# The second norm's factor moved behind the MLP's squares, and the last eighth of w_down without seven-product steps

## The chip, the core and the metric

The kernel runs on one core of a Trainium2 chip. Its engines work side by side, each through its own queue in order: TensorE (PE, with PEld for its weight loads), VectorE (DVE), ScalarE (ACT), GpSimd (POOL) and SyncE (SP), which here only issues loads. Waits between them are semaphores that the framework places from the program's reads and writes; the kernel fixes the order of each queue itself (`manual_schedule`). The metric is the time of one execution in microseconds on the device; the time before is 2056.29 us, the median of three runs from 2054.08 to 2060.91.

## The reference

Two layers over x of 256 tokens by 2048 channels, in float32. Each layer:

```
h = rms_norm(x, norm1_g);  z = h @ w_in            # 2048 x 5120: q, k, v, gate u, gate v
attn = dilated_attention(rotary(q), rotary(k), v)  # 8 heads of 128, three branches merged
gm = chunked_gmlp(gelu(gu), gelu(gv), ...)         # 8 groups, chunks of 128
x = x + concat(attn, gm) @ w_out                   # 2048 x 2048
h2 = rms_norm(x, norm2_g)                          # x * rsqrt(mean(x^2) + 1e-6) * g
x = x + square(relu(h2 @ w_up)) @ w_down           # 2048 x 8192 and 8192 x 2048
```

and a last `rms_norm(x, final_g)`. What the change uses: the norm's factor r is one positive number per token, so relu(r * z)^2 = r^2 * relu(z)^2, and r^2 can be applied to the sums that come out of w_down.

## The kernel before, in words

x lies transposed (channels on the 128 partitions, tokens along the rows), in 16 chunks of 128 x 256. Float32 products are made of three float32r products: each operand is split into a rounded part hi and a rest lo, and hi*hi, lo*hi and hi*lo are added in PSUM. For each block of weights (128 x 1024 floats, 512 KB) SyncE loads `raw` (L156), ScalarE copies it into `hi` (L165), VectorE subtracts to get `lo` (L175), and TensorE uses both. There are `RAW_BUFS` 6, `HI_BUFS` 7 and `LO_BUFS` 6 buffers; a load waits for the raw buffer of the load that stands so many places before it to be free. The main loop at the end of `trunk` walks a list of steps; at each it issues hi copies about six blocks ahead (`high_to`), calls that are due (`run_due`: `soon(n, f)` means n blocks later), lo subtractions about five ahead (`low_to`), loads, and then the step's matmuls and what follows them. So ScalarE and VectorE run ahead of TensorE, but each in the program's order.

The MLP is cut into eighths of 1024 hidden channels. Round e of the list has the 16 up steps of eighth e (four blocks of contraction for each of four pairs of channel chunks, index 0 to 15) and, from e = 1, the down steps of eighth e-1. An up pair ends in `after_up`: VectorE multiplies relu by the factor (L748), ScalarE squares (L749) and writes the hi half (L637), VectorE the lo half (L640). After the fourth pair `sums` makes the differences that a fast product needs. The down product adds into x, 512 output columns at a time by one of two ways:

- four-block steps (24 matmuls of 128x256, `transposed`), 96 matmuls for 512 columns of an eighth; `update` adds the bank to x (L496);
- seven-product steps (`fast`): a 2x2 scheme of seven products instead of eight, two steps of 42 matmuls, 84 for 512 columns. Each needs a top and a bottom load and two sums of them, made in place by VectorE (L216, L217, L220, L221); products in order: top, bottom, bottom, upper sums, upper sums, lower sums, and the seventh after the first matmuls of the next step. Its seven sums of 128x256 gather over eighths before they are combined: group 0 (columns 0 to 511) in aux banks, with its seventh sum alone going through DRAM, groups 1 and 2 through DRAM entirely: ScalarE copies the banks into `stage` (L852, L843) and GpSimd adds it to `far` in DRAM by a DMA (L824). In the group's last eighth (`FINAL`) `far` is added into `stage` instead (L847), VectorE combines the seven into four quarters (`combine`, seven operations of 128x256), TensorE turns them back (L798) and `update` adds them to x.

`ORDER` and `USUAL` say before which index of a round a group's two steps stand: `((11, 14), (1, 2), (6, 7))` is group 0 at 11 and 14, group 1 at 1 and 2, group 2 at 6 and 7. Rounds 2 to 6 use all three groups, round 1 the groups 0 and 1, round 7 too, round 8 group 0 alone. A group that isn't in a round goes by four-block steps there.

## Time and profile before

| | |
|---|---|
| median of three runs | 2056.29 us |
| profiled execution, its own time | 2054.4 us |
| its span | 2052.4 us |
| busy: TensorE / VectorE / ScalarE / GpSimd | 2028.0 / 1617.1 / 1163.7 / 100.4 us |
| mean granted clock | 0.997 |
| DMA | 419.51 MB, mean 204 GB/s |
| L748, 64 times | 44.0 us of VectorE |

The profile's rows give a group as: line, engine, operation, what it writes and reads, shape and count, then busy time and the mean of one, then the engine's idle time just before and what ended it. Matmuls overlap, so the busy time of TensorE says little on its own; the time between the starts of two matmuls says more: 734 matmuls of one round take 83.32 us where nothing is waited for, 0.114 us each. A wait row reads: engine and line that waited, whom it waited for, microseconds in total, times, the longest. A row of the chain of waits has a start, a length and what held the end up.

### The profile page before, as it was taken

The numbers are of one execution on the slowest core, as the hardware profiler recorded it, in microseconds if no ns is written. First come the engines' busy times: TensorE is split into PE (matmuls) and PEld (weight loads), VectorE is DVE, ScalarE is ACT, GpSimd is POOL, SyncE is SP. The second block draws the span as 40 slices with busy tenths as digits, with TensorE's granted clock in tenths as the row PEclk, the third lists the DMA queues.
The fourth block names the chain that finished last, engine by engine and source line by source line (L and its number), as shares of the span: only waits on it lengthen the run. The fifth ranks groups of instructions, "written<-read, shape, count | busy, mean of one in ns | idle before, by whom it ended". The sixth has DMA issues, their size and how long they took to land.

```text
span 2052.4 us, 40724 instructions
## 1 busy us (share of the span) xinstructions
PE 2028.0 (99%) x16810; PEld 1984.3 (97%) x16810; DVE 1617.1 (79%) x2014; ACT 1163.7 (57%) x1535; POOL 100.4 (5%) x130
## 2 busy tenths in 40 slices
PE   9999999999999999999999999999999999999997
PEld 7998999999999999999989989999999999999997
DVE  7666766788889898888875667668889898898896
ACT  7555454556555665565554654545566665665544
POOL 0002300000000000000000033000000000000000
PEclk9999999999999999999999999999999999999999
DMA  8555555566676676666475455565675866757663
GB/s 316 188 165 173 185 189 195 177 223 214 216 227 219 227 214 217 210 220 217 165 237 173 165 183 187 185 202 179 214 232 199 252 207 213 242 192 236 197 220 105
DMA packets 117514, 419.51 MB, mean 204 GB/s; under 512 B 13008, under 2 KB 18640, under 8 KB 117328
## 3 DMA queue, kind: packets, MB, share of 16 engines
q1 hardware_dynamic: 110800, 389.86, 55.4%
q0 software_dynamic: 5376, 24.12, 6.1%
q8 instruction: 131, 2.15, 0.4%
q10 hardware_dynamic: 1152, 2.94, 0.4%
q14 instruction: 55, 0.45, 0.1%
HBM read 394.58 MB, written 22.28 MB: 203 GB/s over the span
## 4 chain that ended last, share of the span: by engine, by line
PE 80%; DVE 11%; ACT 4%; issue 3%; DMA 2%; SPq 0%; DVEq 0%; ACTq 0%
PE acc L399 19%; PE acc L401 19%; PE acc L397 19%; DVE lo L175 4%; PE acc L458 3%; PE acc L456 3%; PE acc L457 3%; ACT hi L165 2%; PE aux L429 2%; PE aux L427 2%; PE aux L430 2%; DMA raw<-in_w 2%; PE acc L429 2%; PE acc L427 2%; PE acc L430 2%
## 5 line engine op out<-in xcount | busy, mean ns | idle before, releaser
L175 DVE TENSOR_TENSOR lo<-raw,hi 128x1024 fp32r<-128x1024 f32 (+1 forms) x821 | 965.6, 1213 | 132.6 <-ACT hi L165 117.7
L165 ACT ACTIVATE hi<-raw 128x1024 fp32r<-128x1024 f32 (+1 forms) x821 | 828.2, 1048 | 415.4 <-DVE raw L217 263.1
L399 PE MATMUL acc<-hs,lo 128*128 128x256 f32 x2816 | 781.5, 278 | 1.7 <-DVE lo L175 1.1
L397 PE MATMUL acc<-hs,hi 128*128 128x256 f32 x2816 | 782.1, 278 | 0.0
L401 PE MATMUL acc<-hs,hi 128*128 128x256 f32 x2816 | 778.9, 277 | 0.0
L399 PEld LDWEIGHTS acc<-hs,lo 128*128 128x128 f32 x2816 | 528.7, 188 | 5.9 <-DVE lo L175 5.3
L397 PEld LDWEIGHTS acc<-hs,hi 128*128 128x128 f32 x2816 | 529.3, 188 | 0.4 <-issue 0.2
L401 PEld LDWEIGHTS acc<-hs,hi 128*128 128x128 f32 x2816 | 528.6, 188 | 0.0
L397 PE MATMUL acc<-half,hi 128*128 128x256 f32 x1280 | 354.6, 277 | 0.0
L399 PE MATMUL acc<-half,lo 128*128 128x256 f32 x1280 | 353.9, 276 | 0.0
L401 PE MATMUL acc<-half,hi 128*128 128x256 f32 x1280 | 353.9, 276 | 0.0
L397 PEld LDWEIGHTS acc<-half,hi 128*128 128x128 f32 x1280 | 240.7, 188 | 0.0
L399 PEld LDWEIGHTS acc<-half,lo 128*128 128x128 f32 x1280 | 240.3, 188 | 0.0
L401 PEld LDWEIGHTS acc<-half,hi 128*128 128x128 f32 x1280 | 240.2, 188 | 0.0
L429 PE MATMUL acc<-lo,shared 128*128 128x256 f32 x384 | 107.2, 279 | 0.0
L430 PE MATMUL acc<-hi,shared 128*128 128x256 f32 x384 | 106.3, 277 | 0.0
L427 PE MATMUL acc<-hi,shared 128*128 128x256 f32 x384 | 106.2, 277 | 0.0
L749 ACT ACTIVATE ar<-ar 128x512 f32<-128x512 f32 x64 | 40.5, 633 | 112.8 <-DVE ar L748 112.7
L456 PE MATMUL acc<-hi,hs 128*128 128x512 f32 x256 | 101.5, 397 | 0.5 <-ACT hs L283 0.5
L458 PE MATMUL acc<-hi,hs 128*128 128x512 f32 x256 | 100.7, 393 | 0.0
L457 PE MATMUL acc<-lo,hs 128*128 128x512 f32 x256 | 99.9, 390 | 0.3 <-DVE lo L175 0.3
L496 DVE TENSOR_TENSOR x<-x,acc 128x512 f32<-128x512 f32 (+1 forms) x73 | 49.3, 675 | 64.4 <-PE acc L401 64.4
(154 smaller groups left out, 2620.4 us busy)
## 6 DMA issues: line engine op xcount, KB each, us to landing
raw<-in_w SPq DMA_DIRECT2D x731, 512.0 KB, 4.7
far<-ar POOLq DMA_DIRECT2D x20, 896.0 KB, 7.7
ar<-far POOLq DMA_DIRECT2D x4, 896.0 KB, 10.1
raw<-in_w SPq DMA_DIRECT2D x10, 256.0 KB, 5.0
x<-in_xT SPq DMA_DIRECT2D x7, 256.0 KB, 5.6
far<-ar POOLq DMA_DIRECT2D x14, 128.0 KB, 6.0
out<-x SPq DMA_DIRECT2D x7, 256.0 KB, 3.1
shared<-in_b_sp ACTq DMA_DIRECT2D x2, 512.0 KB, 8.1
```

What stands on the lines that cost most here:

```text
L165: act.activation(self.h[:, j * m:(j + 1) * m], self.raw[:, j * m:(j + 1) * m], AF.Copy)
L175: vec.tensor_tensor(lo[:, r], self.raw[:, r], self.h[:, r].bitcast(F32), op=OP.subtract)
L397: pe.matmul(o, lhsT=hi, rhs=xs[:, 0, :], start=(k0 + k == 0 and (two or cb == 0)), stop=False, skip_group_check=True)
L399: pe.matmul(o, lhsT=wt.lo[:, k, cb * P:(cb + 1) * P], rhs=xs[:, 0, :], start=False, stop=False, skip_group_check=True)
L401: pe.matmul(o, lhsT=hi, rhs=xs[:, 1, :], start=False, stop=last, skip_group_check=True)
L427: pe.matmul(o[n], lhsT=xh, rhs=hi, start=(p == 0 and k == 0 and n in fresh), stop=False, skip_group_check=True)
L429: pe.matmul(o[n], lhsT=xh, rhs=lo, start=False, stop=False, skip_group_check=True)
L430: pe.matmul(o[n], lhsT=xl, rhs=hi, start=False, stop=(n in last and p == 1 and k == 1), skip_group_check=True)
L456: pe.matmul(ps, lhsT=xh, rhs=hi, start=(k0 + k == 0), stop=False)
L457: pe.matmul(ps, lhsT=xh, rhs=lo, start=False, stop=False)
L458: pe.matmul(ps, lhsT=xl, rhs=hi, start=False, stop=(k0 + k == KC - 1))
L496: vec.tensor_tensor(xj, xj, ps[j][:, 0:S] if alone else pair(ps)[:, j, :], op=OP.add)
```

## The change

1. For eighths 0 to 6 `after_up` is a relu on ScalarE, straight from the bank; the factor n2.R stays on VectorE for eighth 7 alone. `squared` makes r^2 in both layouts, and the sums are multiplied by it later: at once for columns 1024 to 1535 where they go by four-block steps (`after_down`); for columns 1536 to 2047 the sums of eighths 0 to 6 are kept in SBUF (`rest_sums`), multiplied once and added to x (`rest_in`); in `combine` ScalarE scales the four results by token, before they are turned back.
2. Round 8 has no seven-product steps: its eight pairs of columns go by four-block steps in the order `LAST`. Group 0 ends in round 7 (`FINAL` 7), where its steps stand at 6 and 9 instead of 11 and 14; its `combine` works in `stage`, 14 blocks after the second step, and turns back six blocks after that instead of two.
3. A stage leaves, or comes back, in four transfers of up to 512 columns, listed two blocks apart; the last `combine` of groups 1 and 2 stands nine blocks after the last copy instead of five.
4. `RAW_BUFS` 7 and `HI_BUFS` 6 instead of 6 and 7.

VectorE, round 6 of layer 1, at the group-0 step at index 14 (L177 is lo, L218 to L223 the sums of weights, L814 to L822 `combine`, L643 the lo half of an up pair in the changed kernel). Before:

```order
L175 TENSOR_TENSOR lo<-raw,hi 128x1024
L216 TENSOR_TENSOR raw<-raw 128x2x256
L217 TENSOR_TENSOR raw<-raw 128x2x256
L220 TENSOR_TENSOR raw<-raw 128x2x256
L221 TENSOR_TENSOR raw<-raw 128x2x256
L780 TENSOR_TENSOR ar<-ar 128x256
...
L788 TENSOR_TENSOR ar<-ar 128x256
L748 SCALAR_TENSOR_TENSOR ar<-acc_21990,nR 128x512
L175 TENSOR_TENSOR lo<-raw,hi 128x1024
L640 TENSOR_TENSOR half<-ar,half 128x2x256
L175 TENSOR_TENSOR lo<-raw,hi 128x1024 x6
```

and now:

```order
L177 TENSOR_TENSOR lo<-raw,hi 128x1024
L218 TENSOR_TENSOR raw<-raw 128x2x256
L219 TENSOR_TENSOR raw<-raw 128x2x256
L222 TENSOR_TENSOR raw<-raw 128x2x256
L223 TENSOR_TENSOR raw<-raw 128x2x256
L177 TENSOR_TENSOR lo<-raw,hi 128x1024
L643 TENSOR_TENSOR half<-ar,half 128x2x256
L814 TENSOR_TENSOR ar<-ar 128x256
...
L822 TENSOR_TENSOR ar<-ar 128x256
L177 TENSOR_TENSOR lo<-raw,hi 128x1024 x8
```

`combine` and L748 stood between the sums of weights and the lo of the upper sums; now the upper sums' lo follows at once, `combine` stands before the lo of the lower sums, and L748 is gone.

GpSimd at the end of layer 1's MLP, from the last stage of group 1 that leaves (far_90, far_91 and far_92 hold the groups 0, 1 and 2). Before:

```order
L824 DMA far_91<-ar 128x1792
L847 DMA ar<-far_92 128x1792
L824 DMA far_90<-ar 128x256
L847 DMA ar<-far_91 128x1792
L824 DMA far_90<-ar 128x256
L835 DMA ar<-far_90 128x256
```

and now:

```order
L862 DMA far_91<-ar 128x512 x3
L862 DMA far_91<-ar 128x256
L893 DMA ar<-far_92 128x512 x3
L893 DMA ar<-far_92 128x256
L862 DMA far_90<-ar 128x256
L893 DMA ar<-far_91 128x512 x3
L893 DMA ar<-far_91 128x256
L873 DMA ar<-far_90 128x256
```

The queue's order by stage is the same with one sending of group 0 less; each stage is four rows, and nothing else stands between them.

The diff:

```diff
--- before.py
+++ after.py
@@ -51,8 +51,8 @@
 BRANCHES = ((128, 1), (512, 4), (2048, 16))
 NEG = -1.0e30
-RAW_BUFS = 6
-HI_BUFS = 7
+RAW_BUFS = 7
+HI_BUFS = 6
 LO_BUFS = 6
 FRONT = ("cosR", "nr", "rv2", "rt2", "nhalf", "mx", "den")
@@ -60,8 +60,9 @@
-ORDER = {1: ((7, 10), (13, 14)), 7: ((11, 14), (1, 2)), 8: ((0, 2),)}
-FINAL = (8, 7, 6)
+ORDER = {1: ((7, 10), (13, 14)), 7: ((6, 9), (1, 2)), 8: ()}
+FINAL = (7, 7, 6)
+LAST = (4, 6, 8, 10, 0, 2, 12, 14)
 USUAL = ((11, 14), (1, 2), (6, 7))
 WARM = 11
 HALVES = 5
@@ -112,6 +113,7 @@
     inner_flat = ar[:, 0:2048]
     inner = inner_flat.rearrange("p (k t) -> p k t", k=NH)
     stage, stage_one = ar[:, 2048:3840], ar[:, 3840:4096]
+    rest_sums = ar[:, 4096:5120].rearrange("p (k t) -> p k t", k=4)
     def new_shared(dtype):
@@ -364,14 +366,15 @@
         del steps[n:]
         return part
-    def transposed(name, l, row0, nk, col0, ncols, moving, after, between=None, apart=False, of=4):
-        order = [(c, k) for c in range(0, ncols, 256) for k in range(0, nk, 4)]
+    def transposed(name, l, row0, nk, col0, ncols, moving, after, between=None, apart=False, of=4, cols=None):
+        cols = cols or range(0, ncols, 256)
+        order = [(c, k) for c in cols for k in range(0, nk, 4)]
         if between:
             h = nk // 8
             order[h:2 * h], order[2 * h:3 * h] = order[2 * h:3 * h], order[h:2 * h]
@@ -382,7 +385,7 @@
             wt = Sub(name, l, row0 + k0 * P, col0 + c, 4, 256)
             def mm(wt=wt, k0=k0, c=c):
-                two = apart and c == ncols - 256
+                two = apart and c == cols[-1]
                 if k0 == 0:
                     accs[c] = [acc_bank(of=of), acc_bank(of=of)] if two else acc_bank(of=of)
                 ps = accs[c]
@@ -740,12 +743,43 @@
         hid = [[None] for _ in range(8)]
+        def wide(t):
+            return t[:, None, :].to_broadcast([P, 2, S])
+        def squared():
+            n2.spread()
+            n2.r2, n2.R2 = t32("nr2", [2]), t32("nR2", [S])
+            act.activation(n2.r2, n2.r, AF.Square)
+            act.activation(n2.R2, n2.R, AF.Square)
+        def after_down(e, c, ps):
+            if e == 8:
+                update(n3, c, ps, True, last)
+            elif c < 12:
+                vec.tensor_tensor(pair(ps), pair(ps), wide(n2.R2), op=OP.mult)
+                update(n3, c, ps, False, last)
+            elif e == 1:
+                act.activation(rest_sums[:, c - 12:c - 10, :], pair(ps), AF.Copy)
+            else:
+                y = rest_sums[:, c - 12:c - 10, :]
+                vec.tensor_tensor(y, y, pair(ps), op=OP.add)
+        def rest_in(c):
+            y = rest_sums[:, c - 12:c - 10, :]
+            vec.tensor_tensor(y, y, wide(n2.R2), op=OP.mult)
+            vec.tensor_tensor(x[:, c:c + 2, :], x[:, c:c + 2, :], y, op=OP.add)
         def after_up(e):
             def f(c, ps):
                 if hid[e][0] is None:
                     new_half(hid[e])
                 z = inner[:, c // P:c // P + 2, :]
-                vec.scalar_tensor_tensor(z, pair(ps), 0.0, n2.R[:, None, :].to_broadcast([P, 2, S]), op0=OP.max, op1=OP.mult)
+                if e < 7:
+                    act.activation(z, pair(ps), AF.Relu)
+                else:
+                    vec.scalar_tensor_tensor(z, pair(ps), 0.0, wide(n2.R), op0=OP.max, op1=OP.mult)
                 act.activation(z, z, AF.Square)
                 to_half(hid[e][0], c // P, z, True)
                 if c == 768:
@@ -786,17 +820,20 @@
             if o:
                 vec.tensor_tensor(d4, d4, p4, op=OP.subtract)
             vec.tensor_tensor(d7, d7, p5, op=OP.add)
-            wait = 2 if o else 7
-            soon(wait, lambda: turn_back(c, d2, d4, banks[0], o is not None))
-            soon(wait + (1 if o else 2), lambda: turn_back(c + 2, d3, d7, banks[1], o is not None))
-        def turn_back(c, first, second, bank, final):
+            for tt, out in enumerate(((d2, d3), (d4, d7))):
+                for d in out:
+                    act.activation(d, d, AF.Copy, scale=n2.r2[:, tt:tt + 1])
+            wait = 6 if o else 7
+            soon(wait, lambda: turn_back(c, d2, d4, banks[0]))
+            soon(wait + (1 if o else 2), lambda: turn_back(c + 2, d3, d7, banks[1]))
+        def turn_back(c, first, second, bank):
             ps = bank()
             for j in range(2):
                 for tt, src in enumerate((first, second)):
                     o = j * S + tt * P
                     pe.transpose(ps[:, o:o + P], src[:, j * P:(j + 1) * P], ident)
-            soon(1, lambda: update(n3, c, ps, final, last))
+            soon(1, lambda: update(n3, c, ps, False, last))
         def halves(bank):
             return [bank[:, 0:256], bank[:, 256:512]]
@@ -819,21 +856,24 @@
         far = [dp.tile([P, 256 if g == 0 else 7 * 256], F32, name=f"far{l}{g}") for g in range(3)]
-        def put(e, g, src):
-            nc.gpsimd.dma_start(far[g], src, **({} if e == max(g, 1) else {"accum_op": OP.add}))
+        def put(e, g, r):
+            src = stage[:, r] if g else stage_one
+            nc.gpsimd.dma_start(far[g][:, r], src, **({} if e == max(g, 1) else {"accum_op": OP.add}))
         def seventh_out(e, o):
             act.activation(stage_one, o[6], AF.Copy)
-            put(e, 0, stage_one)
+            put(e, 0, slice(0, 256))
         def first_done(e):
             def f(o):
-                if e < 8:
+                if e < 7:
                     soon(5, lambda: seventh_out(e, o))
                 else:
-                    nc.gpsimd.dma_start(inner_flat[:, 1536:1792], far[0])
-                    soon(6, lambda: combine(inner_flat, 0, [aux_bank] * 2, o))
+                    soon(10, lambda: nc.gpsimd.dma_start(stage[:, 1536:1792], far[0]))
+                    soon(14, lambda: combine(stage, 0, [aux_bank] * 2, o))
+                    for i, c in enumerate((12, 14)):
+                        soon(17 + 2 * i, lambda c=c: rest_in(c))
             return f
         def other_done(e, g, banks):
@@ -841,11 +881,16 @@
             def rest(o):
                 act.activation(stage[:, 1536:1792], o[6], AF.Copy)
+                for i in range(4):
+                    soon(2 * i, lambda r=slice(512 * i, min(512 * (i + 1), 1792)): move(r))
+                if e == FINAL[g]:
+                    soon(9, lambda: combine(stage, 4 * g, here))
+            def move(r):
                 if e < FINAL[g]:
-                    put(e, g, stage)
+                    put(e, g, r)
                 else:
-                    nc.gpsimd.dma_start(stage, far[g], accum_op=OP.add)
-                    soon(5, lambda: combine(stage, 4 * g, here))
+                    nc.gpsimd.dma_start(stage[:, r], far[g][:, r], accum_op=OP.add)
             def f(o):
                 for i in (2, 0, 1):
@@ -862,13 +907,14 @@
                 w = 512 * len(ORDER.get(e, USUAL))
                 hidden = [hid[e - 1]]
                 down = collect(transposed, "w_down", l, (e - 1) * 1024, 8, w, D - w, from_tiles(hidden, NH),
-                               lambda c, ps, e=e, w=w: update(n3, (c + w) // P, ps, e == 8, last),
-                               apart=last and e == 8, of=2 if e < 8 else 4)
+                               lambda c, ps, e=e, w=w: after_down(e, (c + w) // P, ps),
+                               apart=last and e == 8, of=2 if e < 8 else 4,
+                               cols=None if e < 8 else [c * P for c in LAST])
                 for g, at in enumerate(ORDER.get(e, USUAL)):
                     banks = []
                     quick += zip(at, collect(fast, "w_down", l, (e - 1) * 1024, 512 * g, hidden,
                                              (lambda g=g, banks=banks: slots_other(g, banks)) if g else slots_first,
-                                             (0, 2, 4, 6) if g or e == 1 else (6,), range(7) if g or e == 8 else (6,),
+                                             (0, 2, 4, 6) if g or e == 1 else (6,), range(7) if g or e == 7 else (6,),
                                              other_done(e, g, banks) if g else first_done(e)))
             quick = dict(quick)
             for i, one in enumerate(up + down):
@@ -878,7 +924,7 @@
         if last:
             hook(base + 4, lambda: act.activation(warm[:, 0:1], ones[:, 0:1], AF.Sqrt))
         hook(base + 1, n2.factor)
-        hook(base + 2, n2.spread)
+        hook(base + 2, squared)
     hooks = {}
```

## The prediction

> **What bounds the kernel now.** I read the page first, then the stretches, TensorE's waits, the chain of waits, the timelines of VectorE and GpSimd, the groups of instructions by form and the DMA issues. The page:
>
> ```profile
> span 2052.4 us, 40724 instructions
> PE 2028.0 (99%) x16810; PEld 1984.3 (97%) x16810; DVE 1617.1 (79%) x2014; ACT 1163.7 (57%) x1535; POOL 100.4 (5%) x130
> ```
>
> TensorE is the bound, so time can only come from fewer matmuls or from its small stalls. The span is 2052.4 us; that execution's own time is 2054.4 us, 1.9 under the median of the runs shown. I cut the MLP into its rounds e (from the first matmul of one to that of the next): rounds 2 to 6, which run the same mixture of steps, first layer 0, then layer 1. Columns: stretch, length, busy time and count of TensorE, its weight loads, VectorE, ScalarE, GpSimd, granted clock, DMA share, GB/s.
>
> ```profile
> 462.24:545.56 83.32, 83.32 (x734) 83.32 (x733) 71.98 (x83) 49.42 (x63) 2.33 (x3) 1.00 0.69 226
> 545.56:631.74 86.18, 84.78 (x734) 83.95 (x733) 75.09 (x87) 51.69 (x66) 2.60 (x3) 1.00 0.68 219
> 631.74:716.48 84.74, 84.45 (x734) 83.74 (x733) 75.09 (x87) 51.72 (x66) 2.58 (x3) 1.00 0.70 222
> 716.48:802.26 85.78, 84.78 (x734) 83.85 (x733) 75.09 (x87) 51.78 (x66) 2.59 (x3) 1.00 0.69 220
> 802.26:893.38 91.12, 88.55 (x742) 87.93 (x741) 78.87 (x95) 51.77 (x65) 2.62 (x3) 0.98 0.64 207
> ...
> 1481.48:1564.80 83.32, 83.32 (x735) 83.32 (x734) 71.99 (x83) 49.42 (x63) 2.32 (x3) 1.00 0.69 226
> 1564.80:1649.60 84.80, 84.45 (x734) 83.83 (x733) 75.08 (x87) 51.63 (x66) 2.56 (x3) 1.00 0.69 222
> 1649.60:1734.24 84.64, 84.36 (x735) 83.68 (x734) 75.08 (x87) 51.77 (x66) 2.54 (x3) 1.00 0.69 223
> 1734.24:1819.59 85.35, 84.38 (x734) 83.67 (x733) 75.07 (x87) 51.77 (x66) 2.55 (x3) 1.00 0.68 221
> 1819.59:1907.91 88.32, 85.41 (x742) 84.70 (x741) 78.88 (x95) 51.69 (x65) 2.58 (x3) 1.00 0.68 214
> ```
>
> Round 2 takes 83.32 us in both layers: 734 matmuls of 0.114 us, without a stall. The same work takes 84.6 to 86.2 us in rounds 3 to 5 and 91.1 and 88.3 us in round 6, which adds eight transposes (742 against 734, about 1.1 us with their hand-over, an estimate). VectorE is busy 75.1 of about 84 us there. Over the whole run TensorE waits for hardly anything else in the MLP:
>
> ```profile
> PE aux L429 <- DVE lo L175: 7.9, 7, 2.4
> PE aux L798 <- DVE ar L787: 1.6, 2, 1.0
> ```
>
> (L429 is the lo product of a seven-product step whose sums sit in an aux bank, the group-0 step at index 14; L798 turns back the last combine.) The largest, in layer 0's round 6: the chain first, then the timelines of VectorE, TensorE, GpSimd and the load queue.
>
> ```profile
> 853.52 8.40 DMA raw<-in_w
> 862.00 1.07 ACT hi L165
> ```
> ```profile
> 863.10 1.23 DVE L175 TENSOR_TENSOR lo<-raw,hi 128x1024 fp32r<-128x1024 f32 x1 [4.46 <-ACT hi L165]
> ...
> 867.02 0.42 DVE L780 TENSOR_TENSOR ar<-ar 128x256 f32<-128x256 f32 x1
> ...
> 869.87 0.68 DVE L748 SCALAR_TENSOR_TENSOR ar<-acc,nR 128x512 f32<-128x512 f32 x1
> 870.47 1.22 DVE L175 TENSOR_TENSOR lo<-raw,hi 128x1024 fp32r<-128x1024 f32 x1
> ```
> ```profile
> 871.74 0.58 PE L429 MATMUL aux<-lo,shared 128*128 128x256 f32 x1 [2.41 <-DVE lo L175]
> ```
> ```profile
> 852.02 0.88 POOL L847 DMA_DIRECT2D ar<-far  x1 [24.14 <-ACT ar L843]
> ```
> ```profile
> 846.67 0.33 SPq L156 DMA_DIRECT2D raw<-in_w  x1
> ```
>
> A stage of 896 KB is fetched at 852.02, the step's top weights were asked for at 846.67, its bottom weights only at 853.52; these land 8.4 us later, VectorE idles 4.46 us, then does combine's seven operations (867.02 to 869.87, 2.85 us) and L748 (0.6 us net) ahead of the lo that TensorE stands waiting for. A stall of that length also costs clock: just behind it the granted clock is 0.50.
>
> ```profile
> 871.50:874.90 3.40, 3.16 (x15) 3.16 (x16) 2.92 (x4) 3.40 (x5) 0.00 (x0) 0.50 0.48 157
> ```
>
> **The change, part by part.** *Round 8 without seven-product steps.* In each layer 84 matmuls become 96: 24 more in all, by 0.114 us: **+2.7 us**, on the path. Eight weight blocks and their sums leave VectorE with them. The last combine moves to round 7's end, its transposes come six steps later instead of two, so their 1.6 us wait for L787 goes: **-1.6**. Its DMA fetch moves on GpSimd's queue past nothing but other stages.
>
> *Relu without the factor.* Prices, by form:
>
> ```profile
> L748 DVE SCALAR_TENSOR_TENSOR ar<-acc,nR 128x512 f32<-128x512 f32 x64 | 44.0, 687 | 53.7 <-PE acc L401 53.7
> L749 ACT ACTIVATE ar<-ar 128x512 f32<-128x512 f32 x64 | 40.5, 633 | 112.8 <-DVE ar L748 112.7
> L852 ACT ACTIVATE ar<-acc 128x512 f32<-128x512 f32 x72 | 37.8, 600 | 29.0 <-PE acc L430 29.0
> L496 DVE TENSOR_TENSOR x<-x,acc 128x512 f32<-128x512 f32 x71 | 48.5, 683 | 62.2 <-PE acc L401 62.2
> L605 ACT ACTIVATE ar<-ar,den 128x256 f32<-128x256 f32 x16 | 7.1, 494 | 0.0
> ```
>
> 56 of the 64 L748 leave VectorE (38.5 us in all, 2.75 a round in rounds 0 to 6) and become 56 relus on ScalarE, by L852's 0.60 us 34 us: busy 57% of the span there, and waiting 112.7 us for L748, so it has the room; without that cover 34 us would be the price. Behind a relu on ScalarE's queue stand the hi copies of the next blocks; before, they stood behind L749, which waited for L748, which waited for the same matmul, so nothing new waits. The factor comes back as eight multiplications of bank sums, four of the kept sums and four additions into x (16 by 0.68, L496's price, = 11 us of VectorE, in rounds 1, 7 and 8, which have two pairs of seven-product steps or none instead of three), and 24 scalings on ScalarE (by L605, 12 us), six or seven steps before the transposes that need them. All at zero on the path. Adding into the kept sums instead of into x costs the same operation.
>
> *Seven raw buffers, six hi.* The load of the bottom block now waits for the lo seven loads back, which is the one that released the load before it, not a lo of the previous seven-product step. In layer 0's round 6 that is the load of 846.67, so the bottom block is asked for some 6 us earlier, is there when VectorE comes to it, and the 4.46 us of idle time end. Bounds for one hi buffer less: nothing where ScalarE follows VectorE, one L165 (1.05 us by its group) per seven-product step where it doesn't; I take nothing.
>
> *Combine three steps later.* In round 6 it moves behind the upper sums' lo. From the end of TensorE's step at index 11 the relu chain and the half's lo take about 2.6 us, combine 2.85, the lower lo 1.2: 6.7 us; TensorE wants it two steps of 2.7 and five products of 0.68 later, 8.8 us. It fits with 2 us to spare.
>
> Together: index 14 and the step behind it should run without a stall in rounds 3 to 6. What stays is the stall at a round's start. VectorE, layer 1, end of round 4 and start of 5:
>
> ```profile
> 1723.56 0.69 DVE L748 SCALAR_TENSOR_TENSOR ar<-acc,nR 128x512 f32<-128x512 f32 x1 [0.74 <-PE acc L401]
> ...
> 1725.61 0.69 DVE L640 TENSOR_TENSOR half<-ar,half 128x512 fp32r<-128x512 f32 x1 [0.23 <-ACT half L637]
> ...
> 1745.52 4.79 DVE L175 TENSOR_TENSOR lo<-raw,hi 128x1024 fp32r<-128x1024 f32 x4
> ```
>
> From L640 on, 1725.61 to about 1750, it works on sums and the two steps at 1 and 2 almost without a break, and it starts when ScalarE has the half. The relu takes L748's place in that chain (0.60 for 0.69), so the burst starts as late as now. The price of it, from the same matmuls at the start of rounds 2 and 4, up to the fourth four-block step:
>
> ```profile
> 1481.48:1499.28 17.80, 17.80 (x159) 17.80 (x158) 13.22 (x15) 10.35 (x13) 0.00 (x0) 1.00 0.64 207
> 1649.60:1668.04 18.44, 18.32 (x159) 18.00 (x158) 16.69 (x19) 13.08 (x17) 0.00 (x0) 1.00 0.48 166
> ```
>
> These 0.64 us I leave in each: rounds 3 to 5 become 83.97 us, round 6, with its transposes, 85.07. Saved against the rows: layer 0 2.21 + 0.77 + 1.81 + 6.05 = 10.8; layer 1 0.83 + 0.67 + 1.38 + 3.25 = 6.1: **-16.9 us**. Round 6's two turned-back updates (2 by 0.68) now fall into round 7's burst: **+1.0** for both layers, between nothing and 2.7.
>
> *A slower pitch.* The same 214 matmuls of round 7 in layer 0 and in layer 1:
>
> ```profile
> 953.20:978.20 25.00, 25.00 (x214) 25.00 (x214) 21.46 (x28) 12.75 (x17) 1.44 (x2) 1.00 0.61 202
> 1967.50:1991.60 24.10, 24.10 (x214) 24.10 (x214) 20.97 (x28) 12.43 (x17) 1.44 (x2) 1.00 0.63 212
> ```
>
> At full granted clock the first is 3.7% slower. By the matmuls' starts it holds from about 818 to 882 (64 us by 3.7% = 2.3, already in the saving) and from 942 to 1012 us (2.5 us), beginning and ending at a stall or transposes. I expect half of these 4.8 us again: 2.4 stay, and since the saving above already counts 2.3 of the 4.8, that leaves **-0.1**.
>
> *Stages in four transfers.* On GpSimd's queue nothing separates them but the copies that they wait for; the queue holds only stages here, and nobody waits for it sooner than ten steps later.
>
> ```profile
> raw<-in_w SPq DMA_DIRECT2D x731, 512.0 KB, 4.7
> far<-ar POOLq DMA_DIRECT2D x20, 896.0 KB, 7.7
> ar<-far POOLq DMA_DIRECT2D x4, 896.0 KB, 10.1
> far<-ar POOLq DMA_DIRECT2D x14, 128.0 KB, 6.0
> ```
>
> Between one transfer's 7.7 us and four by 6.0 (24 us, if they followed one another); each waits only for its own slice, so I take about 8, hidden behind ten steps of 2.7 us. The bytes are the same.
>
> **Sum:** 2.7 - 1.6 - 16.9 + 1.0 - 0.1 = -14.9 on 2054.4: 2039.5 us. The median lay 1.9 over that execution, so I say **2040 us**.
>
> **Rivals.** (a) *The loads stay late.* If the bottom blocks are late because the queues are full (8.4 us against 4.7), not because they are asked for late, index 14 keeps its stalls, less L748's 0.69 in eight rounds (5.5) and about 4 in the rounds 6, where combine stands elsewhere: 2054.4 - 5.5 - 4 - 1.6 + 2.7 + 1 = 2047 us; should the four transfers delay loads further, nothing of the 9.5 is left and it is 2056. For it: the chain goes through that load; against: the load of 846.67 was in time. The Trainium skill ("DMA: Bandwidth & Descriptors", Rules for kernel authors and the section on the anatomy of a SWDGE DMA) says to coalesce small transfers, since each has about 2 us of fixed cost: a stage in four would hold its queue some 6 us longer, an estimate from that page, which would be this rival at its upper end; the rows here, 6.0 us for 128 KB and 7.7 for 896, agree that the fixed part is most of it.
>
> (b) *The bursts shorten too.* Better loads and 2.75 us of VectorE may also clear the starts of rounds 3 to 7: 0.64 by 8, and as much with the 1.0 in the rounds 7, 7.4 us: 2032. Against it: the chain above.
>
> (c) *Slower than before.* Stalls and transposes also end the slow pitch. With the stalls gone TensorE could fall into it at the start of round 3 and stay: 3.7% of a stretch. To eat 14.9 us it must last 400 us more, to be slower by over 0.3% 570 us, nearly rounds 3 to 8 of both layers (some 930 us); then 2039.5 + 930 x 0.036 = 2073. For it: in layer 0 it held 64 and 70 us; against: it began in two of a dozen disturbances, and transposes ended it.
>
> (d) *The change doesn't do what it says*: ScalarE, with relus that wait for TensorE on its queue, delays hi copies as much as VectorE gained: saved only the 1.6, so 2056.
>
> **Chances.** Forecast 0.60, (a) 0.17, (b) 0.13, (c) 0.05, (d) 0.05. A measurement of this kernel can tell about 0.3% (6 us) from no change: faster is under 2050. Forecast, (b) and a third of (a) are faster: 0.79; the rest of (a) and half of (d) are the same: 0.14; slower 0.07. The range goes from 2030, a little under (b)'s 2032, to the upper half of (a), 2053.
>
> **What would show it.** Right: rounds 3 to 5 near 84.0 us in both layers, round 6 near 85, no wait of the lo products (L432 in the changed kernel) for VectorE at index 14, no 0.50 clock in the MLP, no wait for combine at the transposes, VectorE busy about 72 us in rounds 3 to 5. Wrong: index 14 still stalls behind a load, round starts cost over 1 us, or stretches at 0.118 us a matmul without a stall.

## The result, and the profile after

The changed kernel takes 2042.87 us (median of six runs, 2037.9 to 2047.87) beside 2055.62 for the kernel before: a ratio of 0.9934, 95% interval 0.9913 to 0.9954. So it is faster by 0.5 to 0.9%; the forecast was 2040 and faster. The profiled execution took 2044.94 us. Its page:

```profile
span 2042.6 us, 40747 instructions
...
PE 2027.5 (99%) x16834; PEld 1988.6 (97%) x16834; DVE 1579.3 (77%) x1950; ACT 1214.8 (59%) x1613; POOL 156.8 (8%) x200
```

TensorE has its 24 matmuls more and is still the bound; VectorE lost 38 us of work, ScalarE gained 51, GpSimd 56, nearly all for issuing transfers. The rounds 3 to 6, layer 0 and then layer 1, and the rounds 7 and 8 of layer 1 together (stretch, length, then busy time and count of TensorE, weight loads, VectorE, ScalarE, GpSimd, granted clock, DMA share, GB/s):

```profile
545.51:629.35 83.84, 83.79 (x734) 83.52 (x733) 72.78 (x83) 54.48 (x70) 7.88 (x9) 1.00 0.73 225
629.35:715.52 86.17, 86.12 (x734) 85.85 (x733) 73.38 (x83) 54.88 (x70) 7.89 (x9) 1.00 0.71 219
715.52:801.62 86.10, 86.10 (x735) 86.10 (x733) 73.06 (x83) 54.46 (x70) 7.89 (x9) 1.00 0.72 219
801.62:888.39 86.77, 86.77 (x742) 86.77 (x741) 75.95 (x92) 55.91 (x74) 7.96 (x9) 1.00 0.70 217
1560.53:1644.37 83.84, 83.79 (x734) 83.52 (x733) 72.77 (x83) 54.49 (x70) 7.78 (x9) 1.00 0.72 225
1644.37:1728.22 83.85, 83.73 (x734) 83.46 (x733) 72.77 (x83) 54.49 (x70) 7.78 (x9) 1.00 0.73 225
1728.22:1812.09 83.87, 83.82 (x734) 83.54 (x733) 72.79 (x83) 54.49 (x70) 7.77 (x9) 1.00 0.72 225
1812.09:1896.86 84.77, 84.77 (x742) 84.44 (x741) 76.11 (x91) 56.17 (x74) 7.85 (x9) 1.00 0.72 222
1896.86:2029.20 132.34, 131.15 (x1146) 130.36 (x1145) 105.22 (x130) 75.31 (x102) 4.07 (x5) 1.00 0.51 168
```

Layer 1 is what was forecast: 83.85 us where 83.97 was said, 84.77 where 85.07 was said. In layer 0 round 3 is the same, but rounds 4 to 6 are 2.0 to 2.3 us longer, with TensorE busy all the time: no stall, a slower pitch (86.10 us / 735 = 0.117 us a matmul, at a granted clock of 1.00). TensorE's waits:

```profile
PE acc L400 <- ACT hi L167: 2.3, 2, 1.1
PE aux L321 <- DVE nr L347: 1.2, 1, 1.2
PE aux L980 <- DVE warm L976: 1.1, 1, 1.1
PE acc L460 <- DVE lo L177: 0.5, 1, 0.5
```

The 7.9 us for the lo of the aux products and the 1.6 at the transposes are gone. The first row is new: one stall in round 7 of each layer. In layer 1, TensorE, VectorE, and the row of ScalarE that holds the hi copy of the step that waits (the second of the two, by counting copies and steps back from the end of the layer):

```profile
1977.80 0.28 PE L404 MATMUL acc<-half,hi 128*128 128x256 f32 x1
1979.22 0.36 PE L400 MATMUL acc<-half,hi 128*128 128x256 f32 x1 [1.14 <-ACT hi L167]
```
```profile
1976.19 0.42 DVE L822 TENSOR_TENSOR ar<-ar,aux 128x256 f32<-128x256 f32 x1
1976.52 1.22 DVE L177 TENSOR_TENSOR lo<-raw,hi 128x1024 fp32r<-128x1024 f32 x1
1977.66 0.69 DVE L761 TENSOR_TENSOR acc<-acc,nR 128x512 f32<-128x512 f32 x1
1978.38 0.69 DVE L499 TENSOR_TENSOR x<-x,acc 128x512 f32<-128x512 f32 x1
```
```profile
1963.72 2.00 ACT L167 ACTIVATE hi<-raw 128x1024 fp32r<-128x1024 f32 x2
```

The first matmul of the last pair of column chunks (14 and 15, columns 1792 to 2047) starts 1.42 us behind its forerunner, as VectorE finishes with the bank of the pair two before, chunks 10 and 11 (1978.38 + 0.69 = 1979.07). L761, the multiplication by r^2 that came with the change, and L499 of that pair stand behind the last `combine` (L814 to L822). The row names ScalarE's hi, but the hi of this step was there at 1965.7, over 13 us before: it is the bank that TensorE waits for.

### The profile page after: what moved, and what is told of

Its sections match the earlier page's. It is cut to its first block, busy times and chain, and to the rows that moved or that the text cites. A ratio compares the mean times of both kernels' runs of the same rounds, so it can differ in the third digit from the quotient of the medians.

```text
span 2042.6 us, 40747 instructions
## 1 busy us (share of the span) xinstructions
PE 2027.5 (99%) x16834; PEld 1988.6 (97%) x16834; DVE 1579.3 (77%) x1950; ACT 1214.8 (59%) x1613; POOL 156.8 (8%) x200
## 3 DMA queue, kind: packets, MB, share of 16 engines
q1 hardware_dynamic: 110800, 389.86, 56.3%
## 4 chain that ended last, share of the span: by engine, by line
PE 91%; DVE 5%; ACT 2%; issue 1%; DMA 1%; ACTq 0%; DVEq 0%; SPq 0%
PE acc L402 22%; PE acc L404 22%; PE acc L400 22%; PE acc L461 3%; PE acc L459 3%; PE acc L460 3%; PE aux L430 3%; PE aux L433 3%; PE aux L432 3%; PE acc L430 2%; PE acc L432 2%; PE acc L433 2%; DVE lo L177 2%; ACT hi L167 1%; DVE shared L643 1%
## 5 line engine op out<-in xcount | busy, mean ns | idle before, releaser
L167 ACT ACTIVATE hi<-raw 128x1024 fp32r<-128x1024 f32 (+1 forms) x817 | 836.8, 1050 | 516.2 <-DVE raw L219 233.9
L177 DVE TENSOR_TENSOR lo<-raw,hi 128x1024 fp32r<-128x1024 f32 (+1 forms) x817 | 965.0, 1213 | 155.8 <-ACT hi L167 153.6
L400 PE MATMUL acc<-half,hi 128*128 128x256 f32 x1344 | 373.0, 278 | 2.3 <-ACT hi L167 2.3
L402 PE MATMUL acc<-half,lo 128*128 128x256 f32 x1344 | 372.0, 277 | 0.0
L404 PE MATMUL acc<-half,hi 128*128 128x256 f32 x1344 | 372.0, 277 | 0.0
L400 PEld LDWEIGHTS acc<-half,hi 128*128 128x128 f32 x1344 | 252.8, 188 | 2.6 <-ACT hi L167 2.6
L402 PEld LDWEIGHTS acc<-half,lo 128*128 128x128 f32 x1344 | 252.6, 188 | 0.0
L404 PEld LDWEIGHTS acc<-half,hi 128*128 128x128 f32 x1344 | 252.4, 188 | 0.0
L862 POOL DMA_DIRECT2D far<-ar x92 | 74.7, 983 | 1168.2 <-ACT ar L865 620.7
L432 PE MATMUL acc<-lo,shared 128*128 128x256 f32 x384 | 107.4, 280 | 0.0
L643 DVE TENSOR_TENSOR half<-ar,half 128x512 fp32r<-128x512 f32 x72 | 49.7, 691 | 67.8 <-ACT half L640 67.6
```

Source lines behind the costliest of these rows:

```text
L167: act.activation(self.h[:, j * m:(j + 1) * m], self.raw[:, j * m:(j + 1) * m], AF.Copy)
L177: vec.tensor_tensor(lo[:, r], self.raw[:, r], self.h[:, r].bitcast(F32), op=OP.subtract)
L400: pe.matmul(o, lhsT=hi, rhs=xs[:, 0, :], start=(k0 + k == 0 and (two or cb == 0)), stop=False, skip_group_check=True)
L402: pe.matmul(o, lhsT=wt.lo[:, k, cb * P:(cb + 1) * P], rhs=xs[:, 0, :], start=False, stop=False, skip_group_check=True)
L404: pe.matmul(o, lhsT=hi, rhs=xs[:, 1, :], start=False, stop=last, skip_group_check=True)
L432: pe.matmul(o[n], lhsT=xh, rhs=lo, start=False, stop=False, skip_group_check=True)
```

## The experiments

Rounds are compared by the same matmuls in each trace; an asterisk marks a round that ran for over 10 us at the slower pitch. "Block" is when SyncE asks for the bottom block of group 0's step at index 14 and when it has landed, in us from the start of layer 1's round 4; "lo waits" is TensorE's row for the lo of the aux products (L429 before, L432 after), with the number of times.

| kernel | raw/hi | factor | a stage in | block | lo waits, us | layer 1, rounds 3, 4, 5, 6 | median |
|---|---|---|---|---|---|---|---|
| before | 6/7 | VectorE | 1 | 50.2 to 57.1 | 7.9, 7 times | 84.8, 84.6, 85.4, 88.3 | 2055.62 |
| round8_only | 6/7 | VectorE | 1 | 50.2 to 57.9 | 12.3, 10 | 85.4, 85.5, 85.2, 90.9 | 2062.54 |
| factor_only | 6/7 | later | 1 | 49.5 to 56.3 | 7.4, 6 | 83.9, 83.8, 86.2*, 90.4 | 2057.52 |
| both_back | 6/7 | VectorE | 4 | 50.2 to 55.1 | 0.2, 1 | 84.0, 84.0, 86.3*, 86.8* | 2042.37 |
| bufs_back | 6/7 | later | 4 | 49.5 to 54.1 | none | 83.9, 83.9, 83.9, 84.8 | 2039.51 |
| before_bufs | 7/6 | VectorE | 1 | 44.1 to 48.6 | none | 84.0, 86.3*, 86.1*, 86.4* | 2040.79 |
| one_transfer | 7/6 | later | 1 | 43.3 to 47.9 | none | 83.9, 83.9, 84.1, 84.8 | 2038.62 |
| factor_back | 7/6 | VectorE | 4 | 44.1 to 51.8 | none | 84.0, 86.3*, 86.1*, 86.8* | 2040.4 |
| changed, again | 7/6 | later | 4 | 43.3 to 52.3 | none | 83.9, 83.9, 83.9, 84.8 | 2038.0 |

(`combine` of groups 1 and 2 stands nine blocks after the last copy where a stage goes in four, and in one_transfer; otherwise five. The medians come from several batches of runs; a ratio is to the kernel before in the same batch.)

### One part put back: the buffers, the factor

```diff
-RAW_BUFS = 7
-HI_BUFS = 6
+RAW_BUFS = 6
+HI_BUFS = 7
```

> The changed kernel with six raw and seven hi buffers again, as before; everything else of the change stays. Theory (the seventh raw buffer brings the bottom block of index 14 in time): the wait of L432 for VectorE's lo at index 14, gone with the change, comes back in rounds 3 to 6 of both layers, some 1 to 2 us in layer 0 and about half of that in layer 1, without L748 and combine in between; rounds 3 to 5 are 84.3 to 85.5 us again instead of 83.85, and the kernel 3 to 8 us slower than the changed one, 2046 to 2051. Rival (what counted is the work that left VectorE, L748 and combine between the sums of weights and the lo): index 14 stays free of stalls, layer 1's rounds 3 to 5 stay within 0.2 us of 83.85, and the time is that of the changed kernel within 2 us.

Measured: 2039.51 us, ratio 0.9926 (0.9910 to 0.9943); no wait for the lo, layer 1's rounds at 83.85. The theory failed, and by its wording the rival held.

```diff
...
-                vec.tensor_tensor(pair(ps), pair(ps), wide(n2.R2), op=OP.mult)
...
-            vec.tensor_tensor(y, y, wide(n2.R2), op=OP.mult)
...
-                if e < 7:
-                    act.activation(z, pair(ps), AF.Relu)
-                else:
-                    vec.scalar_tensor_tensor(z, pair(ps), 0.0, wide(n2.R), op0=OP.max, op1=OP.mult)
+                vec.scalar_tensor_tensor(z, pair(ps), 0.0, wide(n2.R), op0=OP.max, op1=OP.mult)
...
-            for tt, out in enumerate(((d2, d3), (d4, d7))):
-                for d in out:
-                    act.activation(d, d, AF.Copy, scale=n2.r2[:, tt:tt + 1])
```

> The changed kernel with the factor back at the relu on VectorE in all eight eighths; r squared, its scalings and its multiplications are left out, so that the result is the reference's as before. Buffers, combine's place, round 8 and the four transfers stay. Theory (the loads' lateness set the stalls, VectorE's 2.75 us a round only lengthened them by 0.69 each): index 14 keeps a margin of 2 us against 0.69 more, so no stall comes back there; rounds 3 to 5 of layer 1 stay at 83.8 to 84.1 us, VectorE is busy 75 us in them instead of about 72; the time is 0 to 3 us above the changed kernel's, 2043 to 2046. Rival (VectorE's work was the cause): the waits of the lo products at index 14 return, rounds 3 to 6 grow by 0.7 us and more each, and the time is 8 to 12 us above, 2051 to 2055.

Measured: 2040.4 us, ratio 0.9930 (0.9912 to 0.9948); rounds without the slower pitch 83.95 to 83.96. The theory held: VectorE's 2.75 us a round are worth 0.1 us a round here (rounds 7 and 8, where the factor comes back, are another matter; see the unused differences below). Neither of the two parts is needed where the other stands: either each is enough, or a third part does it.

### The stages, and the set filled up

```diff
-                for i in range(4):
-                    soon(2 * i, lambda r=slice(512 * i, min(512 * (i + 1), 1792)): move(r))
+                move(slice(0, 1792))
```

> The changed kernel with a stage leaving or coming back in one transfer of 896 KB again, issued when the seventh sum is copied; buffers, factor, combine's place and round 8 stay as changed. Both the buffers and the factor could be put back singly without a stall at index 14 coming back (layer 1's rounds 3 to 5 stayed at 83.85 and 83.96 us). New theory (the single transfer, a read and a write of 896 KB within some 8 us, held up the weight loads that ran beside it, and the four transfers took that away): with one transfer rounds 3 to 5 of layer 1 are 84.6 us or more again, with waits of L432 for the lo at index 14, and the kernel is 6 to 12 us above the changed one's 2038, 2044 to 2050. Rival (buffers, factor and combine's place each give the margin alone, the prediction's cost of nothing for the four transfers is right): rounds 3 to 5 stay at 83.85, the time within 2 us of 2038.

Measured: 2038.62 us, ratio 0.9903 (0.9884 to 0.9923); the rounds stay at 83.85 (one at 84.13). The transfers are not the only cause either.

both_back has both edits of the last section; round8_only has all three and `combine` five blocks after the last copy; before_bufs is the kernel before with only its two numbers of buffers changed; factor_only is round8_only with the factor moved.

> The changed kernel with six raw and seven hi buffers and the factor at the relu on VectorE together; the four transfers, combine's place and round 8 stay as changed, the result is the reference's. Theory of the four transfers: still no stall at index 14, layer 1's rounds 3 to 5 at 83.85 to 84.0 us, time 2036 to 2044 by how long the slower pitch lasts. Rival (either the buffers or the factor is needed, each stands in for the other): the waits of the lo products at index 14 come back as before, rounds 3 to 5 are 84.6 us and more, round 6 over 87, time 2046 to 2052.

> Only the part of the change that concerns round 8 (eight pairs of columns by four-block steps, group 0 ending in round 7, columns 1536 to 2047 kept and added at once); six raw and seven hi buffers, the factor on VectorE, one transfer a stage and combine five blocks after the last copy as before. Theory of the four transfers, and the prediction too: rounds 3 to 6 are as before (layer 1: 84.8, 84.6, 85.4, 88.3 us), 24 more matmuls cost 2.7 us and the last combine's wait of 1.6 goes: within 2 us of the kernel before, 2053 to 2057. Rival (the stalls came from what round 8 and group 0 had, not from buffers, factor or transfers): the rounds 3 to 6 are 83.85 to 84.8 us and the time is 2037 to 2045.

> The kernel before with seven raw and six hi buffers and nothing else changed. The prediction's reason (the bottom block of index 14 was asked for late because a raw buffer was missing): index 14's stalls mostly go, rounds 3 to 5 of layer 1 are 83.9 to 84.2 us, the time 2042 to 2048. Theory of the four transfers: one transfer of 896 KB still holds up the loads; rounds 3 to 5 stay at 84.6 to 85.4 us, the waits of L429 for the lo stay at 5 us or more in all, and the time within 3 us of 2054.

> Round 8 as changed and the factor moved behind the squares; six raw and seven hi buffers, one transfer a stage and combine five blocks after the last copy as before. It completes the set: the buffers alone (on the kernel before) and the four transfers with the later combine (on the round-8 kernel) each took the stalls of rounds 3 to 5 away. Theory (the stall is a late load: in the round-8 kernel the load of the bottom block was asked for 64.9 us into layer 1's round 4, 54.1 with a seventh raw buffer, 62.1 with four transfers, 60.5 with four transfers and the factor moved; the factor is thus worth 1.6 us of it and the transfers 2.8): with the factor alone it is asked for at about 63.2 us, layer 1's rounds 3 to 5 are 84.0 to 84.6 us instead of 85.2 to 85.5, and some waits of L432 for the lo stay, 1 to 5 us in all against 12.3. Rival (VectorE's work is what counts): no wait is left and rounds 3 to 5 are 83.85.

Measured:

- both_back 2042.37 us (two runs), ratio 0.9921 (0.9894 to 0.9947), without lo waits to speak of and with 171 us at the slower pitch: the theory of the four transfers held.
- before_bufs 2040.79 us (two runs), 0.9913 (0.9884 to 0.9942): the prediction's reason holds by itself.
- round8_only 2062.54 us, 1.0024 (1.0011 to 1.0037): this part alone makes the kernel slower, by more than either side expected.
- factor_only 2057.52 us, 1.0013 (1.0000 to 1.0026), with no stall in layer 1's rounds 3 and 4, as the rival had it, but 7.4 us of waits in the others, which neither side had. The load that its expectation times (64.9 us in round8_only) is a later one; the bottom block is the one asked for at 50.2.

What round8_only waits for, in round 4 of layer 1: GpSimd, the load queue, ScalarE, and three stretches (columns as above):

```profile
1699.00 0.84 POOL L851 DMA_DIRECT2D far<-ar  x1 [23.29 <-ACT ar L872]
```
```profile
1700.50 4.87 SPq L158 DMA_DIRECT2D raw<-in_w  x5
```
```profile
1708.27 1.06 ACT L167 ACTIVATE hi<-raw 128x1024 fp32r<-128x1024 f32 x1 [5.02 <-DMA raw<-in_w]
```
```profile
1690.00:1700.00 10.00, 10.00 (x90) 10.00 (x89) 8.64 (x11) 7.41 (x11) 0.84 (x1) 1.00 0.63 220
1700.00:1703.00 3.00, 3.00 (x29) 3.00 (x28) 3.00 (x4) 3.00 (x4) 0.00 (x0) 1.00 0.97 146
1703.00:1706.00 3.00, 3.00 (x29) 3.00 (x28) 2.61 (x3) 0.26 (x1) 0.00 (x0) 1.00 0.95 231
```

The stage of group 2 leaves when ScalarE has copied the seventh sum (L872), and 1.5 us later five weight loads are asked for, the bottom block of index 14 first. The DMA engines go from 63% busy to 95% and more, while the bytes moved fall at first, from 220 to 146 GB/s. Whether it is the adding into DRAM that costs them time, no run tests. The block takes 7.7 us; ScalarE stands 5.02 us for it, VectorE behind ScalarE, and TensorE stands at the lower sums' lo. The same place in both_back:

```profile
1677.58 2.62 POOL L851 DMA_DIRECT2D far<-ar  x3 [14.37 <-ACT ar L886]
1686.49 0.85 POOL L851 DMA_DIRECT2D far<-ar  x1 [6.29 <-ACT ar L872]
```
```profile
1692.97 1.06 ACT L167 ACTIVATE hi<-raw 128x1024 fp32r<-128x1024 f32 x1 [2.21 <-PE aux L433]
```

Three of the four transfers need no seventh sum and leave once the banks are copied (39.8 us into the round; the single one left at 48.7). Only 128 KB go at the old place, and the block, asked for at the same 50.2, takes 4.9 us; ScalarE stands 2.21 us instead of 5.02. So the parts take one stall away from different ends. The four transfers make the load quick. The seventh raw buffer has it asked for 6 us sooner, so that it has landed before the stage is in its way (48.6). The moved factor leaves the block nearly as late (56.3) and only shortens VectorE's way from it to the lo: enough in layer 1, not in layer 0 (84.72 and 84.90 us in rounds 4 and 5). Round 6 takes 84.77 us with all parts and about 90 with neither buffers nor transfers. A remainder of 1 us shows in both_back (85.83 in layer 0, hardly at the slower pitch); before_bufs has 86.58 there, of which 58 us ran at the slower pitch, about 2 us longer for it. What the later `combine` brings wasn't tried alone.

### The unused differences

```diff
-                    later(1, 1.5, sums)
+                    if e < 7:
+                        later(1, 1.5, sums)
```

> The changed kernel without the differences of the last eighth's hidden channels and their hi and lo halves (four operations of sums, and parts), which nothing reads since round 8 has no seven-product steps. Theory (in round 7 VectorE does these and then the last combine, so that the banks of index 10 are freed late, and TensorE waits 1.3 us for a bank at the columns of index 14, in each layer): these two stalls are gone, round 7 is 1.0 to 1.5 us shorter in each layer, the time 2 to 3 us lower where the slower pitch stays where it was. Rival (the wait is for the hi copy that the profile names, or for combine alone): the two stalls stay within 0.3 us, and the time is within 1 us of the changed kernel's.

Measured: 2037.35 us, ratio 0.9921 (0.9900 to 0.9941). Its waits, and its rounds 7 and 8 of layer 1:

```profile
PE aux L321 <- DVE nr L347: 1.2, 1, 1.2
PE aux L981 <- DVE warm L977: 1.1, 1, 1.1
PE acc L460 <- DVE lo L177: 0.3, 1, 0.3
```
```profile
1896.52:2027.17 130.65, 130.53 (x1146) 130.18 (x1145) 100.15 (x121) 73.16 (x98) 4.07 (x5) 1.00 0.53 170
```

Both stalls are gone (the indexes 10 and 14 of that expectation are column chunks) and rounds 7 and 8 are 1.7 us shorter (130.65 for 132.34): the theory held, and the hi that the row named was not the cause, as its time above says. The medians, 0.65 us apart from the changed kernel's beside it, don't resolve these 3.4 us: this profiled execution ran 325 us at the slower pitch.

The differences are only half of the cause: the stall needs the moved factor too. All four kernels that have the moved factor and these differences wait 1.1 us there in each layer (the changed kernel in both its profiles, bufs_back, one_transfer, factor_only). The three that have round 8 and the differences, but the factor on VectorE (factor_back, both_back, round8_only), don't. VectorE at the same place in factor_back, and rounds 7 and 8 of layer 1 in both_back:

```profile
1975.64 1.22 DVE L177 TENSOR_TENSOR lo<-raw,hi 128x1024 fp32r<-128x1024 f32 x1
1976.78 0.68 DVE L499 TENSOR_TENSOR x<-x,acc 128x512 f32<-128x512 f32 x1
```
```profile
1894.77:2025.60 130.83, 130.78 (x1146) 130.25 (x1145) 102.50 (x126) 71.83 (x94) 4.09 (x5) 1.00 0.54 174
```

No multiplication stands ahead of L499 here, nor ahead of that of the pair before; the bank is free at 1977.46, and TensorE comes to it at 1977.76, 0.30 us later. Two multiplications of 0.73 us, from one start to the next, would make it 1.16 us late, and 1.14 is the wait of the changed kernel. So they and the differences make the bank late together; without either there is no stall. Where the factor comes back, it thus costs the changed kernel about 1.5 us a layer (132.34 beside 130.83 us). The medians can't show this (factor_back 2040.4, the changed kernel beside it 2038.0), as the profiled execution of factor_back ran some 280 us at the slower pitch.

### The slower pitch

> The changed kernel once more, to see where TensorE's slower pitch (0.118 us a matmul instead of 0.113 at a granted clock of 1.00) lies in another execution. Theory (it is set by the program: it begins at the stall behind a round's first group-1 step and ends at the transposes of the combined groups): the same stretches as in the first profile, about 643 to 882 and 903 to 945 us, none in layer 1, and the same time within 2 us. Rival (it begins at any of these stalls by chance): other stretches, of another total length, and the time differs from the first profile's 2044.9 us by 3.7% of the difference in that length, up to 15 us either way.

Measured: 2038.0 us, ratio 0.9930 (0.9908 to 0.9952), single times 2037.75 to 2046.34. Its rounds 4 to 6 of layer 0:

```profile
629.75:713.60 83.85, 83.80 (x734) 83.52 (x733) 72.78 (x83) 54.51 (x70) 7.89 (x9) 1.00 0.73 225
713.60:797.45 83.85, 83.80 (x735) 83.53 (x733) 72.86 (x83) 54.50 (x70) 7.88 (x9) 1.00 0.72 225
797.45:882.22 84.77, 84.72 (x743) 84.45 (x742) 76.06 (x91) 56.20 (x74) 7.96 (x9) 1.00 0.71 222
```

The same program, and in place of the first profile's 282 us at the slower pitch it has two stretches of 10 us in the rounds 7. The theory fell; where the slower pitch lies is chance. It took 7.2 us less (2044.94 to 2037.75). In no_last_sums it sits in layer 1:

```profile
1551.39:1637.56 86.17, 86.12 (x735) 85.85 (x733) 73.38 (x83) 54.90 (x70) 7.78 (x9) 1.00 0.72 219
1723.65:1809.74 86.09, 86.09 (x734) 86.09 (x733) 72.94 (x83) 54.75 (x70) 7.77 (x9) 1.00 0.72 219
```

### Two groups moved at the round's start

start_later and start_split stand without the unused differences too; start_23, made after them, moves group 1 alone in the rounds of three groups.

```diff
-USUAL = ((11, 14), (1, 2), (6, 7))
+USUAL = ((11, 14), (2, 3), (7, 8))     # start_later; round 7: ((6, 9), (2, 3))
+USUAL = ((11, 14), (1, 3), (6, 7))     # start_split; round 7: ((6, 9), (1, 3))
+USUAL = ((11, 14), (2, 3), (6, 7))     # start_23; round 7: ((7, 10), (2, 3))
```

> The changed kernel without the unused differences of the last eighth, and with group 1's two steps before the indexes 2 and 3 of a round instead of 1 and 2, group 2's before 7 and 8 instead of 6 and 7 (group 1's also in round 7). Theory (VectorE's burst at a round's start, the differences, their halves and the two steps' sums and lo, ends about half a microsecond after TensorE wants it, and that stall is also where the slower pitch begins): with 2.7 us more the two gaps of 0.2 and 0.33 us near index 2 go, rounds 3 to 5 are 83.3 to 83.4 us, no stretch at 0.118 us a matmul begins there, and the time is 2026 to 2031 us, with little spread. Rival (what VectorE has to do moves along with the steps, so the burst only ends later, and group 0 at 11 now collides with group 2 at 8): rounds stay at 83.8 us or grow, time 2035 or more.

> The changed kernel without the unused differences of the last eighth, and with a four-block step more between group 1's two steps (before the indexes 1 and 3 instead of 1 and 2, in round 7 too); all else as changed. Theory (only the second step's sums and lo are late, by about half a microsecond): the gaps at a round's start go or shrink below 0.2 us in all, rounds 3 to 5 are 83.3 to 83.5 us, the time 2027 to 2032. Rival (the first step is late too, and the seventh sums' banks are held one step longer): a gap of at least 0.2 us stays at the first step, and the slower pitch still begins there; time 2031 to 2040.

> The changed kernel without the unused differences of the last eighth, group 1's two steps before the indexes 2 and 3 instead of 1 and 2 in every round that has three groups, group 2's left at 6 and 7; in round 7 group 1 at 2 and 3 and group 0 at 7 and 10 instead of 1, 2 and 6, 9. Theory (with both groups later, the gaps near index 2 were gone, no slower pitch began, and what was lost came from group 2's second step, which stood ahead of index 8, where the next pair of columns wants the bank that this step still holds, 0.86 us a round, and in round 7 from group 0 at 6 behind group 1 at 3, 2.5 us): rounds 2 to 5 are 83.3 to 83.4 us, round 6 84.2 to 84.3, rounds 7 and 8 together about 130 us, no or hardly any slower pitch; the time is 2025 to 2030 us with a spread under 4 us. Rival (with one step less between the groups VectorE, which then has group 1's and group 2's sums closer together, or the stage, which group 2 refills, is late at index 6 or 7): a new gap of 0.3 us or more in each round, rounds 83.7 us or more, time 2031 to 2040.

Measured: start_later 2042.7 us (0.9937, 0.9915 to 0.9958), start_split 2047.19 (0.9956, 0.9940 to 0.9971) and start_23 2042.72 (0.9939, 0.9925 to 0.9954). A wait of start_later, its rounds 2 and 3 of layer 1, and those of start_23:

```profile
PE acc L400 <- ACT ar L898: 6.9, 10, 0.7
```
```profile
1472.25:1556.53 84.28, 83.59 (x735) 83.40 (x733) 69.54 (x78) 54.44 (x70) 6.60 (x9) 1.00 0.72 224
1556.53:1640.80 84.27, 83.58 (x734) 83.39 (x733) 72.84 (x83) 54.81 (x69) 7.79 (x9) 1.00 0.75 224
```
```profile
1472.71:1557.09 84.38, 84.11 (x735) 83.61 (x734) 69.54 (x78) 54.35 (x70) 6.63 (x9) 1.00 0.71 224
1557.09:1641.45 84.36, 84.08 (x734) 83.67 (x733) 72.87 (x83) 54.74 (x69) 7.80 (x9) 1.00 0.73 223
```

In start_later the gaps near index 2 went, as expected, and no stretch at the slower pitch is left in its trace (its four times lie within 0.82 us); but 0.9 us a round were lost at group 2, where the next pair of columns waits for ScalarE to copy a bank (L898), so that the rounds grew, as the rival had it. In start_split, too, the gaps near index 2 went, but gaps of 0.5, 0.2 and 0.3 us came at group 2's steps instead, and the rounds take 84.4 us: slower than either side expected. With group 2 left at 6 and 7 (start_23) that wait goes and VectorE is late there instead (gaps of 0.5 and 0.3 us at index 6 and 7): the rival, in each round, 1.0 us instead of 0.53. None of the three beats the changed kernel; no_last_sums has the lowest median, not resolved from it.

## Why the prediction was right, and where it wasn't

By the segments of the two profiles: rounds 3 to 6 of layer 1 fell by 343.1 - 336.3 = 6.8 us (6.1 forecast, with the round-start stall at 0.64; it is 83.85 - 83.32 = 0.53), those of layer 0 by 347.8 - 342.9 = 4.9 (10.8 forecast), and the rounds 7 and 8 grew by 1.5 in layer 1 and 0.7 in layer 0 (2.1 together forecast). The sum is -9.5 where -14.9 was said, on an execution that fell by 9.46. The median fell by 12.75, and an execution nearly without the slower pitch (`again`, 2037.75) by 16.65 against the same 2054.4: the saving came where it was forecast, but how near a time comes to the 2040 is in part the luck of the pitch. The step that failed is "All at zero on the path" for the factor's return.

- *Index 14 and round 6, -16.9*: right, and a little short. Without the slower pitch layer 0's rounds 3 to 6 take 336.3 us too, 11.5 less than before.
- *The reason given for it*: half right. "The load of the bottom block now waits for the lo seven loads back" ... "and the 4.46 us of idle time end" is what before_bufs shows by itself (asked for at 44.1 instead of 50.2 us into round 4). The wrong step was "hidden behind ten steps of 2.7 us" and with it the price of nothing for *stages in four transfers*: a single stage is what makes that load slow, and sending it in four took the stall of rounds 3 to 5 from the round-8 kernel by itself (`combine` isn't run in those rounds). Counted as a marginal price beside the other parts, nothing is right (2038.62 against 2038.0), and so is nothing for the buffers (2039.51). The gain belongs to no single part: the buffers bring 17.6 us alone (before_bufs) and the transfers with the later `combine` 20.2 from round8_only (both_back), so adding up would count it more than twice.
- *Rival (a)*, that the loads are late because the queues are full: true of why they land late, false of what follows, since a load asked for earlier passes ahead of the stage. Beside its upper end the prediction set the Trainium skill ("DMA: Bandwidth & Descriptors", Rules for kernel authors), which says to coalesce many small transfers into one large one. GpSimd does pay for the four (26.1 us for 32 sends in one_transfer, 74.7 for 92), but off the path. For the load the runs go both ways: asked for at 43.3, the block takes 7.9 and 9.0 us beside four transfers (the changed kernel's two profiles) and 4.6 with one (one_transfer), without harm, since it lands in time either way; asked for at 50.2 it takes 4.9 beside four and 7.7 with one.
- *Round 8 (+2.7), transposes (-1.6), turned-back updates (+1.0)*: the wait at the transposes went. But the sum is right by luck. In both_back, with this part and the factor on VectorE, rounds 7 and 8 of layer 1 take as long as before (130.83 beside 130.82 us), so this part cost nothing there, where 1.0 a layer was forecast; which of the three terms was too high isn't shown. What the changed kernel lost is the stall of the next item, against which stands slower pitch in layer 0's round 7, 2.5 us before and some 0.7 now. With the loads late this part costs more: round8_only is 0.1 to 0.4% slower than before, and its rounds 7 and 8 of layer 1 take 134.4 us, 1.8 of them a wait for the lo of group 0's second step, now at index 9.
- *Factor (nothing on the path)*: right for what it takes away, 0.1 us a round of gain; VectorE is busy 72.8 us in rounds 3 to 5, about 72 was said. Wrong for what comes back: of the eight multiplications of bank sums, "All at zero on the path", the two in each layer's round 7 stand on VectorE ahead of the read that frees a bank, and with the differences that nothing uses any more they make TensorE wait for that bank, about 1.5 us a layer. The prediction looked at what the last `combine` waits for and who waits for it, and not at the bank sums behind it in VectorE's queue.
- *A slower pitch, -0.1*: this term was mis-sized, and no profile ahead of the change could have sized it. The profiled execution lost 2.3 + 2.2 + 2.0 + 0.7 = 7.2 us to it against `again`; 2.4 were forecast to stay. Rival (c) described it (it begins at a round's start and lasts), but not at its size: 282 us in this execution, 325 at the most seen, not 570.
- *Rival (b)*: the bursts did not shorten; the 0.53 us stayed. *Rival (d)*: no relu delays a hi copy that TensorE waits for in the changed kernel.

## What to carry to other kernels

Before an edit of a combined change is priced at nothing, ask what it is worth alone: edits that each loosen the same late transfer have one gain between them, which here either of two delivers alone, and the parts that cost (here round 8, slower alone) live on it. When a transfer is late, look at what else moves at that moment and at what it waits for: here a stage waited for 128 KB of its last slice and so fell together with five weight loads. Work that is moved has to be priced where it lands: two multiplications of 0.7 us delayed a bank at the one place where a long run of other work stands beside them. Where single executions of one kernel differ by 10 us, compare the same stretches of two traces before the medians.

## What was not expected of the hardware

TensorE has two steady paces for the same matmuls at the same granted clock: 734 of them in 83.32 us, or 735 in 86.10. By the starts of the matmuls, 12 of the 13 stretches over 30 us in the changed kernel and its variants with group 1 at 1 and 2 (before_bufs among them) set in between 12.4 and 15.3 us into a round, at the two gaps that stand there, one within group 1's second step and one right behind it. In most other rounds the slower pitch shows for some 4 us at the same gaps and ends by itself; whether it stays is chance. The long stretches ended at turned-back transposes, sometimes only at the second set, or, in kernels that kept other stalls, at one of those. In a round that runs wholly at the slower pitch the gaps of its start vanish, so that it loses 2.24 us, not 2.78. The trace doesn't show a cause.

Also, the engine named in a wait row was wrong in both layers: the wait is put down to ScalarE's hi (L167), whose copy for that step had ended 13 us before; taking work from VectorE ended it.
